# Loading two token rows of a weighted expert sum on 15 DMA engines in place of 16

## The chip, the cores and the metric

The kernel runs on one core of a Trainium2 chip. The metric is the time of the device in microseconds (us), from the start to the end of one execution. The core has five engines with instruction streams of their own: TensorE (PE in the profile), VectorE (DVE), ScalarE (ACT), GpSimd (POOL) and SyncE (SP), which here only issues transfers. Sixteen DMA engines move data between the device's memory (HBM) and the on-chip memory of 128 partitions.

## The reference

Each of 16 x 1024 tokens has eight rows of 512 numbers, one per expert, and eight weights. The output is the weighted sum over the experts.

```python
batch, seq, n_experts, expert_dim = 16, 1024, 8, 512
# expert_outputs: (batch, seq, n_experts, expert_dim), combine_weights: (batch, seq, n_experts)
weights = combine_weights[..., np.newaxis]
return np.sum(expert_outputs * weights, axis=2).astype(np.float32)
```

In float32 the input is 268 MB and the output 34 MB, and each number read is used once.

## The kernel before

The 16384 tokens are laid over the 128 partitions: each partition works on 128 of them, and "token i" below is the i-th of every partition at once, so one token is 128 rows of 16 KB (eight experts of 512 float32). A ring of ten tokens holds the loaded rows. A transfer brings up to four tokens; towards the end they get smaller.

```python
    G = 8
    SLOTS = 10
    PE_TOKENS = 8
    PE_EXPERTS = 3

    x = expert_outputs.rearrange("b s e d -> (b s) e d").rearrange(
        "(n p g) e d -> n p g e d", p=P, g=G
    )
    # ... (weights and output in the same way)
    ring = one.tile([P, SLOTS, E, D], fp32, name="ring")
    acc = one.tile([P, 2 * G, D], fp32, name="acc")
    # ...
    loads = []
    BULK = 112
    t = 0
    while t < BULK:
        m = min(4, SLOTS - t % SLOTS, G - t % G)
        loads += [(t, m, 0, E)]
        t += m
    for t in range(BULK, T_P - 2, 2):
        loads += [(t, 2, 0, E)]
    loads += [(T_P - 2, 1, 0, 4), (T_P - 2, 1, 4, 8)]
    loads += [(T_P - 1, 1, 0, 3), (T_P - 1, 1, 3, 5), (T_P - 1, 1, 5, 7), (T_P - 1, 1, 7, 8)]

    def load_until(t):
        nonlocal loaded
        while loaded < len(loads) and loads[loaded][0] + loads[loaded][1] <= t:
            i, m, e0, e1 = loads[loaded]
            n, g, s = i // G, i % G, i % SLOTS
            if (e0, e1) == (0, E):
                dst, src = ring[:, s : s + m], x[n, :, g : g + m]
            else:
                dst, src = ring[:, s, e0:e1], x[n, :, g, e0:e1]
            pin(nc.sync.dma_start(out=dst, in_=src))
            loaded += 1
```

For all tokens but the last eight, ScalarE makes the first term (row of expert 0 times its weight) and VectorE adds the other seven, one instruction each. For the last eight, TensorE makes the terms of three experts by multiplying with a diagonal matrix of the weights, and VectorE adds five.

```python
    for i in range(0, T_P, 2):
        load_until(i + SLOTS)
        for k in (i + 2, i + 3):
            if k < T_P:
                first(k)              # ScalarE's term, or TensorE's three
        for e in range(E):
            for k in (i, i + 1):
                term(k, e)            # VectorE: acc = ring * weight + acc
        end = i + 2
        if end <= T_P - G and end % G == 0:
            store(end - G, G, nc.scalar)
        # ... (stores of the last eight tokens: 4, 2, 1 and 1)
```

A load waits until the ring's places that it writes have been read by VectorE and ScalarE. Loads go through SyncE's queue, most stores through ScalarE's.

Of the kernel before, what the change touches and what calls it, by code (L numbers as in the profile page):

```python
# [1 line left out]

# [5 lines left out]


@with_exitstack  # L10
def kernel(
    ctx: ExitStack,
    tc: tile.TileContext,
    expert_outputs: bass.AP,
    combine_weights: bass.AP,
    out: bass.AP,
):

    nc = tc.nc
    fp32 = mybir.dt.float32
    mult, add = mybir.AluOpType.mult, mybir.AluOpType.add
    pin = tc.keep_in_program_order

    B, S, E, D = expert_outputs.shape
    T = B * S
    P = 128
    G = 8
    N = T // (P * G)
    T_P = N * G
    SLOTS = 10
    PE_TOKENS = 8
    PE_EXPERTS = 3

    x = expert_outputs.rearrange("b s e d -> (b s) e d").rearrange(
        "(n p g) e d -> n p g e d", p=P, g=G
    )
    w = combine_weights.rearrange("b s e -> (b s) e").rearrange(
        "(n p g) e -> p n (g e)", p=P, g=G
    )
    o = out.rearrange("b s d -> (b s) d").rearrange("(n p g) d -> n p g d", p=P, g=G)

    one = ctx.enter_context(tc.tile_pool(name="one", bufs=1))
    diag_pool = ctx.enter_context(tc.tile_pool(name="diag_pool", bufs=12))  # L50
    ps_pool = ctx.enter_context(
        tc.tile_pool(name="ps_pool", bufs=4, space=bass.MemoryType.PSUM)
    )

    ring = one.tile([P, SLOTS, E, D], fp32, name="ring")
    acc = one.tile([P, 2 * G, D], fp32, name="acc")
    w_t = one.tile([P, T_P, E], fp32, name="w_t")
    ident = one.tile([P, P], fp32, name="ident")


    loads = []
    BULK = 112
    t = 0
    while t < BULK:
        m = min(4, SLOTS - t % SLOTS, G - t % G)
        loads += [(t, m, 0, E)]
        t += m
    for t in range(BULK, T_P - 2, 2):
# [3 lines that stand above are left out]
    loaded = 0  # L72
# [7 lines that stand above are left out]
                dst, src = ring[:, s : s + m], x[n, :, g : g + m]  # L80
            else:
                dst, src = ring[:, s, e0:e1], x[n, :, g, e0:e1]
            pin(nc.sync.dma_start(out=dst, in_=src))  # L83
            loaded += 1

    sums = {}

    def first(i):

        s, a = i % SLOTS, i % (2 * G)  # L90
        if i < T_P - PE_TOKENS:
            pin(nc.scalar.mul(out=acc[:, a], in_=ring[:, s, 0], mul=w_t[:, i, 0:1]))  # L92
            return
        ps = ps_pool.tile([P, D], fp32, name="ps")
        for e in range(PE_EXPERTS):
            diag = diag_pool.tile([P, P], fp32, name="diag")
            pin(nc.scalar.mul(out=diag, in_=ident, mul=w_t[:, i, e : e + 1]))  # L97
            nc.tensor.matmul(  # L98
                ps, lhsT=diag, rhs=ring[:, s, e], start=e == 0, stop=e == PE_EXPERTS - 1
            )  # L100
        sums[i] = ps

    def term(i, e):
        s, a = i % SLOTS, i % (2 * G)
        if i < T_P - PE_TOKENS:
            before, e0 = acc[:, a], 1
        else:
            before, e0 = (sums[i] if e == PE_EXPERTS else acc[:, a]), PE_EXPERTS
        if e >= e0:
            pin(  # L110
                nc.vector.scalar_tensor_tensor(  # L111
                    out=acc[:, a],
                    in0=ring[:, s, e],
                    scalar=w_t[:, i, e : e + 1],
                    in1=before,
                    op0=mult,
                    op1=add,
                )
            )

    def store(i, m, queue):
        n, g, a = i // G, i % G, i % (2 * G)
        pin(queue.dma_start(out=o[n, :, g : g + m], in_=acc[:, a : a + m]))

    pin(nc.sync.dma_start(out=w_t.rearrange("p (n g) e -> p n (g e)", g=G), in_=w))  # L125
    make_identity(nc, ident)
    load_until(SLOTS - 2)
    for i in (0, 1):
        first(i)
# [4 lines that stand above are left out]
                first(k)  # L134
        for e in range(E):
            for k in (i, i + 1):
                term(k, e)
# [3 lines that stand above are left out]
        elif end == T_P - 4:  # L141
            store(end - 4, 4, nc.scalar)
        elif end == T_P - 2:
            store(end - 2, 2, nc.sync)
        elif end == T_P:
            store(end - 2, 1, nc.sync)
            store(end - 1, 1, nc.sync)


# [1 line left out]
_INS = ['expert_outputs', 'combine_weights']  # L151
_OUTS = [((16, 1024, 512), 'float32')]


# [23 lines left out]
```

## Time and profile before

| | |
|---|---|
| time, median of 3 (lowest, highest) | 719.63 us (719.17, 720.88) |
| span of the profiled execution | 718.5 us |
| VectorE busy | 585.6 us (81%), 880 instructions |
| ScalarE busy | 86.7 us (12%) |
| TensorE busy | 28.0 us (4%), in the last 50 us |
| moved by DMA | 302.59 MB, 421 GB/s over the span |
| a load of four tokens, from issue to landing | 35.6 us, median of 19 |
| one VectorE term | 746 ns, 128x512 |

The busy share of an engine says how much of the span it worked, not whether it was waited for. The profile's table of stages gives busy time per engine in a stretch of the span and, in its last two columns, the share of the 16 DMA engines that were busy and the rate. The chain of waits follows the work that ended last back to what released it, step by step. Each DMA queue has a row with its packets, its megabytes and the share of the sixteen engines' span that its packets took. Queue 1 is SyncE's and queue 10 ScalarE's; queue 14 brings instructions. The trace also records when each of the sixteen shares of a transfer had landed.

### The profile page before, as it was taken

How to read it: one execution, taken by the hardware profiler on the slowest of the kernel's cores; microseconds unless marked ns; L12 is line 12 of the kernel's file. 1: busy time of each engine (PE TensorE's matmuls, PEld its weight loads, DVE VectorE, ACT ScalarE, POOL GpSimd, SP SyncE). 2: the span in 40 equal slices, each digit the busy share in tenths (PEclk: the TensorE clock that was granted, in tenths of full speed). 3: DMA queues.
4: the chain of work that ended last, by engine and by line, in shares of the span. 5: the costliest groups of instructions: out<-in, count | busy, mean ns of one | idle time of the engine just before them, and what ended most of it. 6: DMA issues, size and time to landing. Idle time of an engine off the chain costs nothing.

```text
span 718.5 us, 1363 instructions
## 1 busy us (share of the span) xinstructions
PE 28.0 (4%) x48; PEld 11.4 (2%) x48; DVE 585.6 (81%) x880; ACT 86.7 (12%) x145; POOL 0.7 (0%) x6
## 2 busy tenths in 40 slices
PE   0000000000000000000000000000000000000374
PEld 0000000000000000000000000000000000000131
DVE  0499888799697979897789787879897799997647
ACT  0210101111001110101110011111101101102210
POOL 0000000000000000000000000000000000000000
PEclk9999999999999999999999999999999999999967
DMA  9999999999999999999999999999999999999991
GB/s 372 441 427 420 423 438 420 455 406 462 423 425 440 449 405 436 447 431 440 429 415 453 431 425 440 422 430 447 424 441 435 434 416 436 436 431 434 427 405 73
DMA packets 11577, 302.59 MB, mean 421 GB/s; under 512 B 3120, under 2 KB 3120, under 8 KB 4016
## 3 DMA queue, kind: packets, MB, share of 16 engines
q1 hardware_dynamic: 9264, 270.01, 87.3%
q10 hardware_dynamic: 2304, 32.51, 10.6%
q14 instruction: 9, 0.07, 0.0%
HBM read 268.96 MB, written 33.55 MB: 421 GB/s over the span
## 4 chain that ended last, share of the span: by engine, by line
DMA 58%; DVE 36%; PE 2%; ACT 1%; issue 1%; DVEq 0%; SPq 0%; ACTq 0%
DMA ring<-in_expert_outputs_dram 58%; DVE acc L111 36%; PE ps L98 2%; ACT acc L92 1%; ACT L92 0%; DVEq L173 0%; SPq L125 0%; SPq L83 0%; ACTq L92 0%; DVEq L111 0%
## 5 line engine op out<-in xcount | busy, mean ns | idle before, releaser
L111 DVE SCALAR_TENSOR_TENSOR acc<-ring,w_t,acc 128x512 f32<-128x512 f32 x872 | 580.1, 746 | 111.6 <-ACT acc L92 111.6
L92 ACT ACTIVATE acc<-ring,w_t 128x512 f32<-128x512 f32 x120 | 77.6, 711 | 556.6 <-DMA ring<-in_expert_outputs_dram 556.5
L98 PE MATMUL ps<-ring,diag 128*128 128x512 f32 x48 | 28.0, 748 | 679.9 <-DMA ring<-in_expert_outputs_dram 675.7
L98 PEld LDWEIGHTS ps<-ring,diag 128*128 128x128 f32 x48 | 11.4, 245 | 695.6 <-issue 694.1
L111 DVE SCALAR_TENSOR_TENSOR acc<-ring,w_t,ps 128x512 f32<-128x512 f32 x8 | 5.9, 745 | 18.2 <-PE ps L98 18.2
L97 ACT ACTIVATE diag<-ident,w_t 128x128 f32<-128x128 f32 x24 | 7.9, 390 | 29.3 <-PE ps L98 21.8
L92 ACT ACT_TABLE_LOAD x1 | 1.3, 1283 | 25.9 <-DMA ring<-in_expert_outputs_dram 25.9
masks.py:199 POOL TENSOR_SCALAR_AFFINE_SELECT ident<-ident 128x128 f32<-128x128 f32 x1 | 0.3, 292 | 0.1
masks.py:197 POOL MEMSET ident<- 128x128 f32 x1 | 0.2, 205 | 0.3 <-POOLq L162 0.3
L162 POOL MEMSET const-bfloat16-1.0<- 128x1 bf16 x1 | 0.1, 102 | 0.0
L162 POOL MEMSET const-uint8-127<- 128x1 uint8 x1 | 0.1, 102 | 0.0
L162 POOL MEMSET const-float32-0.0<- 128x1 f32 x1 | 0.1, 98 | 0.2 <-issue 0.2
L162 POOL MEMSET const-float32-1.0<- 128x1 f32 x1 | 0.1, 98 | 0.0
## 6 DMA issues: line engine op xcount, KB each, us to landing
ring<-in_expert_outputs_dram SPq DMA_DIRECT2D x19, 4096.0 KB, 35.6
out_dram<-acc ACTq DMA_DIRECT2D x15, 2048.0 KB, 21.9
ring<-in_expert_outputs_dram SPq DMA_DIRECT2D x2, 1024.0 KB, 40.6
ring<-in_expert_outputs_dram SPq DMA_DIRECT2D x2, 512.0 KB, 25.9
out_dram<-acc ACTq DMA_DIRECT2D x1, 1024.0 KB, 7.7
ring<-in_expert_outputs_dram SPq DMA_DIRECT2D x1, 768.0 KB, 41.8
w_t<-in_combine_weights_dram SPq DMA_DIRECT2D x1, 512.0 KB, 4.1
out_dram<-acc SPq DMA_DIRECT2D x1, 512.0 KB, 2.7
```

Source lines behind the costliest of these rows:

```text
L92: pin(nc.scalar.mul(out=acc[:, a], in_=ring[:, s, 0], mul=w_t[:, i, 0:1]))
L97: pin(nc.scalar.mul(out=diag, in_=ident, mul=w_t[:, i, e : e + 1]))
L98: nc.tensor.matmul(ps, lhsT=diag, rhs=ring[:, s, e], start=e == 0, stop=e == PE_EXPERTS - 1)
L111: nc.vector.scalar_tensor_tensor(out=acc[:, a], in0=ring[:, s, e], scalar=w_t[:, i, e : e + 1], in1=before, op0=mult, op1=add,)
L162: nc = _bacc.Bacc("TRN2", target_bir_lowering=False, num_devices=1)
```

## The change

Tokens 48 and 72 are loaded alone, and each in four pieces: partitions 0 to 119, then 120, then 121 and 122, then 123 to 127. A transfer of 120 partitions is meant to run on 15 DMA engines with eight partitions each, so that the sixteenth has nothing to do for it[...]. The neighbours of these tokens in the order of loading are cut differently for it: tokens 48 and 49 were one load and are now two (the first in four pieces), and 72-75 and 76-79 become 72, 73, 74-77 and 78-79. The computation and the stores are the same.

```diff
@@ -36,6 +36,7 @@
     SLOTS = 10
     PE_TOKENS = 8
+    SHORT = (48, 72)
     PE_EXPERTS = 3
@@ -63,6 +64,8 @@
         m = min(4, SLOTS - t % SLOTS, G - t % G)
+        if t in SHORT or t - 1 in SHORT:
+            m = 1
         loads += [(t, m, 0, E)]
         t += m
@@ -80,7 +83,10 @@
-            pin(nc.sync.dma_start(out=dst, in_=src))
+
+            parts = (0, 120, 121, 123, P) if i in SHORT else (0, P)
+            for p0, p1 in zip(parts, parts[1:]):
+                pin(nc.sync.dma_start(out=dst[p0:p1], in_=src[p0:p1]))
             loaded += 1
```

## The prediction

> **What bounds the kernel now.** I read the stages first (busy time of each engine per stretch, granted clock, share of the 16 DMA engines that is busy, and what they moved), then the DMA queues on the page.
>
> ```profile
> core 0: us, PE busy (x) PEld busy (x) DVE busy (x) ACT busy (x) POOL busy (x), PEclk, DMA share, GB/s
> 100.00:300.00 200.00, 0.00 (x0) 0.00 (x0) 168.00 (x254) 24.47 (x38) 0.00 (x0) 1.00 1.00 432
> 300.00:500.00 200.00, 0.00 (x0) 0.00 (x0) 170.17 (x257) 23.25 (x36) 0.00 (x0) 1.00 1.00 434
> 500.00:690.00 190.00, 14.35 (x24) 5.83 (x24) 159.00 (x239) 25.48 (x48) 0.00 (x0) 0.98 1.00 431
> 690.00:700.00 10.00, 5.79 (x8) 2.53 (x8) 6.28 (x10) 1.86 (x6) 0.00 (x0) 0.68 1.00 410
> 700.00:707.00 7.00, 7.00 (x17) 3.04 (x16) 4.78 (x8) 0.00 (x0) 0.00 (x0) 0.97 0.13 53
> 707.00:718.50 11.50, 0.85 (x2) 0.02 (x1) 8.40 (x13) 0.00 (x0) 0.00 (x0) 0.66 0.24 91
> ...
> q1 hardware_dynamic: 9264, 270.01, 87.3%
> q10 hardware_dynamic: 2304, 32.51, 10.6%
> q14 instruction: 9, 0.07, 0.0%
> ```
>
> Until 700 us the DMA engines are busy the whole time (share 1.00); VectorE, the busiest compute engine, has 168 us of work in 200. So the transfers set the pace. A 64 KB load packet takes 2.418 us in the packet records, 27.1 GB/s for one engine, and 16 of these are 434 GB/s: the rate in the table. But from 700 to 707 us the share is 0.13, two engines' worth in the mean. Something is still moving when nearly all have finished.
>
> What that is, the completion marks tell: each transfer leaves sixteen in the trace, one per share. I list them for some loads (tokens, and when the 1st, 8th, 15th and 16th share landed, us):
>
> ```
> tokens   8- 9    52.85   53.26   54.67   54.90
> tokens  48-49   271.26  271.65  273.35  273.80
> tokens  72-75   411.58  412.01  413.67  415.06
> tokens  96-99   542.20  542.62  544.26  547.64
> tokens 124-125  687.55  688.02  689.81  694.02
> token  127 end  697.61  698.03  699.82  706.39
> ```
>
> Fifteen shares land within 1.8 to 2.3 us of each other all the way; some nine come early, the rest up to 2 us later. The sixteenth falls behind, from 0.2 us after the fifteenth to 4.2 at tokens 124-125 and 6.6 at the end. The marks have no engine number, but it is one engine, for its lag grows in equal steps. The packets of the queue of kind "instruction" (8 KB each) start at 70.3, 157.1, 250.0, 278.1, 355.6, 443.6, 538.9, 586.6 and 631.9 us. After those at 157, 250, 356, 444, 539 and 632 one load packet is about 0.65 us longer, and with the fetch's own 0.31 one share is later by 0.96 to 0.98. They come some 95 us apart, which is 128 VectorE instructions of 0.746 us: VectorE's instruction stream, fetched through one DMA engine. Six steps of 0.97 are 5.8; with its place at the start (0.5 after the first) 6.4, and 694.02 - 687.55 is 6.47.
>
> Last, the end of the chain of waits (start, length, what):
>
> ```profile
> 682.63 7.44 PE ps L98 x12
> 690.07 0.02 issue
> 690.09 4.07 DVE acc L111 x6
> 694.16 0.10 issue
> 694.27 8.44 PE ps L98 x12
> 702.71 0.03 issue
> 702.74 4.79 DVE acc L111 x8
> ```
>
> TensorE starts tokens 124-127 at 694.27. The chain names VectorE, but the matmul waits for several semaphores: the PSUM buffer it needs from VectorE was read at 674.3 (token 120), and the load of tokens 124-125 landed at 694.02. So the late engine's share releases it. From there to the end all is compute: 718.5 - 694.0 = 24.5 us (24 matmul passes in 13.6 us, the rest of VectorE's terms, a store). The last pieces of token 127, landed at 706.39, are needed only after 710 and bind nothing. What counts is when tokens 124-125 are complete.
>
> [...]
>
> **The change part by part.** Bytes, VectorE, ScalarE and TensorE instructions stay as they are.
>
> *Issue.* Tokens 48-49 become 5 loads in place of 1, tokens 72-79 seven in place of 2: 9 more issues of 0.33 us on SP, 3 us on an idle sequencer. Loads wait about 35 us from issue to landing, so the queue has some 30 us of work at any time, and this is hidden. The eight completion counters rotate faster; I followed who reuses which. The closest is token 73's load, whose counter belonged to tokens 64-67, landed by 371.5 us; its buffer comes free at about 370. A us or two, hidden too.
>
> *Taken from engine 15.* Eight rows of 16 KB per token. A 16 KB packet of the stores takes 0.611 us, so 8 x 0.611 = 4.9 us per token, 9.8 us for both. If the late engine is 15, it goes from 6.47 us behind the first to 3.3 ahead of it.
>
> *Given to others.* [...] Engine 0: 2 x 3 x 0.611 = 3.7 us; engine 1: 2.4; the others 1.2.
>
> *Sum.* The load of tokens 124-125 is complete when its last engine is. If engine 0 is among the early ones, that is 687.55 + 3.7 + 0.2 = 691.4, beside 689.8 for the late fifteen: 694.0 - 691.4 = 2.6 us gained, and as only compute follows, the end moves as much: 717.0. If the single row is spread over 16, engine 0 gets 2.06 rows per token, 2.5 us, and the landing is 690.1: 3.9 gained, 715.7.
>
> **Rivals.** *Engine 0 is one of the later group:* 687.55 + 2.3 + 3.7 = 693.5, only 0.5 gained, 719.1. The uneven split 1, 2, 5 [...] suggests that it was fitted to engines with slack; this speaks against.
>
> *The late engine is not 15:* if it is one that gets nothing, 719.6; if it is engine 0, 719.6 + 3.7 = 723.3. [...]
>
> [...] Two in step would then need twice the 4.9 us. In the worst case 9.8 us for both tokens on nearly all engines, less about twice their offset (up to 2 us) per token: tokens 124-125 at 698 to 701, a time of 724 to 727. Nothing in the profile before speaks for or against it, as all its transfers have 128 rows. I give it a quarter.
>
> *Already hidden:* if the end hung on VectorE rather than on that landing, nothing would move. VectorE idles 3.63 us before 699.77 and 2.22 before 702.74, both waits on TensorE, so there is no such reserve.
>
> **Range and chances.** About half for 715.5 to 717.5, a quarter for 718.5 to 720.5, a quarter for 721 to 727. I take 717.6, a little above the sum, with 714.9 to 723.5. Two per cent are 14.4 us; nothing here reaches that, save a conflict that disturbs neighbouring loads too.
>
> **What would show it.** Right: the sixteenth mark is no longer apart, the spread at tokens 124-125 under 4 us, their landing near 691, and the low DMA share after 700 gone. The marks of the 120-row loads spread no wider than others. Wrong engine: the lag of 6.5 is still there or has become 10. Conflict: the first fifteen shares land later after tokens 48 and 72, by up to 5 us each, and packets of 16 KB take about 1.2 us where 0.61 was expected.

## The result, and the profile after

The changed kernel is slower: 738.36 us (median of 4 runs, 737.94 to 740.65) beside 720.25 (719.17 to 721.10). The ratio is 1.0259, with a 95% interval of 1.0232 to 1.0286. The prediction of 717.6 us, with 714.9 to 723.5 as its range, does not hold.

The table of stages of the changed kernel, with the columns as before (busy time of each engine, granted clock, share of the 16 DMA engines that is busy, GB/s):

```profile
100.00:300.00 200.00, 0.00 (x0) 0.00 (x0) 163.57 (x246) 22.02 (x34) 0.00 (x0) 1.00 1.00 418
300.00:500.00 200.00, 0.00 (x0) 0.00 (x0) 158.47 (x238) 22.13 (x34) 0.00 (x0) 1.00 1.00 413
500.00:690.00 190.00, 1.72 (x2) 0.84 (x3) 167.57 (x252) 26.22 (x46) 0.00 (x0) 1.00 1.00 433
690.00:700.00 10.00, 6.72 (x11) 2.47 (x9) 3.99 (x6) 3.15 (x9) 0.00 (x0) 1.00 0.99 428
700.00:711.00 11.00, 7.08 (x12) 2.79 (x12) 6.44 (x11) 0.00 (x0) 0.00 (x0) 0.84 0.97 411
711.00:736.70 25.70, 13.34 (x24) 5.56 (x24) 16.57 (x25) 1.86 (x6) 0.00 (x0) 0.71 0.34 135
```

The DMA engines are as busy as before (share 1.00), but between 100 and 500 us they move less: 418 and 413 GB/s, where it was 432 and 434. After 500 us the rate is the old one. So the time goes where tokens 48 and 72 pass, and it goes in transfers that take longer, not in waiting for something to transfer. Five-microsecond windows around token 48 show it; first the kernel before, then the changed one:

```profile
265.00:270.00 5.00, 0.00 (x0) 0.00 (x0) 5.00 (x9) 1.09 (x2) 0.00 (x0) 1.00 1.06 459
270.00:275.00 5.00, 0.00 (x0) 0.00 (x0) 5.00 (x9) 1.12 (x2) 0.00 (x0) 1.00 1.05 452
```

```profile
265.00:270.00 5.00, 0.00 (x0) 0.00 (x0) 3.74 (x6) 2.56 (x4) 0.00 (x0) 1.00 1.00 223
270.00:275.00 5.00, 0.00 (x0) 0.00 (x0) 5.00 (x9) 0.00 (x0) 0.00 (x0) 1.00 0.99 226
```

For ten microseconds the engines are fully busy at half the rate. The packet records agree: the 512 load packets of 16 KB (tokens 48 and 72, and 49 and 73 queued right behind them) last 1.15 us in the median, where 0.61 was expected.

The same loads as in the prediction's list of completion marks (when the 1st, 8th, 15th and 16th share landed, us), as far as both kernels have them:

```
                         1st      8th     15th     16th
tokens  50-53 before  291.85   292.27   294.57   294.96
              after   296.22   300.69   302.55   304.70
tokens  80-83 before  455.09   455.51   457.18   459.54
              after   463.55   472.06   474.79   478.01
tokens 124-125 before 687.55   688.02   689.81   694.02
              after   699.87   703.35   707.26   712.42
```

After token 48 the middle of the engines is 8.4 us late, after token 72 16.5, at the end 15.3. One share is ahead of the next by 3.3 and then 7.1 us. I take it for the engine that the two loads of 120 rows leave out (each left completion marks for fifteen shares, not sixteen), the prediction's engine 15; eight missing rows per token would make at most 4.9 and 9.8 (an estimate, 8 and 16 packets of 0.611 us). No record names an engine, so every engine number here and in the recorded texts is the author's. And the sixteenth share is still apart from the rest: at tokens 124-125 it lands 9.1 us after the eighth, where it was 6.0. The last engine was not relieved.

The end of the chain of waits of the changed kernel hangs on that landing as before:

```profile
666.22 46.20 DMA ring<-in_expert_outputs_dram
712.42 0.24 issue
712.66 8.21 PE ps L104 x12
720.87 0.02 issue
720.89 4.79 DVE acc L117 x8
```

From 712.42 to the end of the span, 736.7, it is 24.3 us (24.5 before). The landing came 18.4 us later and the time is 18.1 us longer. Two questions follow: why all engines lose some 15 us, and why the late one loses another 3.

### The profile page after: what moved, and what is told of

Read it like the earlier page. It is cut to its first block, busy times and chain, and to the rows that moved or that the text cites. A ratio compares the mean times of both kernels' runs of the same rounds, so it can differ in the third digit from the quotient of the medians.

```text
span 736.7 us, 1389 instructions
## 1 busy us (share of the span) xinstructions
PE 28.9 (4%) x48; PEld 11.7 (2%) x48; DVE 585.7 (80%) x880; ACT 87.0 (12%) x145; POOL 0.7 (0%) x6
## 3 DMA queue, kind: packets, MB, share of 16 engines
q10 hardware_dynamic: 2304, 32.51, 10.3%
## 4 chain that ended last, share of the span: by engine, by line
DMA 60%; DVE 36%; ACT 1%; issue 1%; PE 1%; DVEq 0%; SPq 0%; ACTq 0%
DMA ring<-in_expert_outputs_dram 60%; DVE acc L117 36%; PE ps L104 1%; ACT acc L98 1%; ACT L98 0%; DVEq L179 0%; SPq L131 0%; SPq L89 0%; DVEq L117 0%; ACTq L98 0%
```

## The experiments

The prediction's rival of engines that hinder each other when they write at the same moment (two in step, twice the time) fits the halved rate of 223 and 226 GB/s, but so would others: the order of the reads in HBM, an odd number of engines, the small pieces, the finer cut. The first four runs tell them apart; their expectations give first what this conflict would make, then what the others would.

**Loads alone.** Eight one-token loads ahead of the kernel before, each starting when the one before has landed, and five tiny transfers behind the load of tokens 118-119 that count the engines off.

```diff
+    marks = one.tile([16, 5, 128], fp32, name="marks")
 ...
             pin(nc.sync.dma_start(out=dst, in_=src))
             loaded += 1
+            if i == 118:
+                for k in range(1, 6):
+                    pin(nc.sync.dma_start(out=marks[:k, k - 1], in_=x[0, :k, 0, 0, :128]))
 ...
+    row = x[0, :, 0]
+    for dst, src in (
+        (ring[:, 0], row),
+        (ring[0:120, 0], row[0:120]),
+        (ring[0:126, 0], row[0:126]),
+        (ring[0:64, 0], row[0:64]),
+        (ring[0:120, 0], x[0, :15].rearrange("p g e d -> (p g) e d")),
+        (ring[0:127:9, 0], row[0:127:9]),
+        (ring[0:15, 0], row[0:15]),
+        (ring[:, 0], row),
+    ):
+        pin(nc.sync.dma_start(out=dst, in_=src))
     load_until(SLOTS - 2)
```

> The kernel before, with eight loads of one token ahead of its own, each starting when the one before has landed, so that all engines begin together: 128 rows, 120, 126, 64, 120 from HBM rows that lie one after the other, 15 rows nine partitions apart, the first 15 rows, 128 again. Also five tiny transfers of 1, 2, 3, 4 and 5 rows behind the load of tokens 118-119. [...] packets of 16 KB take 0.61 us in the loads of 128, in that of 126 [...] and of 15 spaced rows; 1.2 us in both loads of 120 and in that of 64; the first 15 rows[...], about 2.4 us. So 120 rows take 4.9 us longer than 128, and 64 rows as long as 128. HBM theory (the order of the reads there collides): the load of 120 from consecutive rows is fast again, and 64 and 15 rows are like 128. Odd-count theory (a transfer that isn't 16 shares is slow): 120, 126 and both loads of 15 rows are slow, 64 isn't. The tiny transfers tell the late engine's number: I expect its late mark in those of 4 and 5 rows and not in those of 1 to 2[...].

The time of the whole, 783.26 us in one run, contains the added loads and says nothing. The windows from each load's issue to its last landing (second column, us) do; in order 128 rows (the first of all, beside the load of the weights), 120, 126, 64, 120 from consecutive HBM rows, 15 spaced, the first 15, and 128 again:

```profile
1.24:10.89 9.65, 0.00 (x0) 0.00 (x0) 0.00 (x0) 0.00 (x0) 0.06 (x1) 1.00 0.80 272
10.91:22.55 11.64, 0.00 (x0) 0.00 (x0) 0.00 (x0) 0.00 (x0) 0.00 (x0) 1.00 0.78 169
22.57:30.58 8.01, 0.00 (x0) 0.00 (x0) 0.00 (x0) 0.00 (x0) 0.00 (x0) 1.00 0.67 258
30.59:38.04 7.45, 0.00 (x0) 0.00 (x0) 0.00 (x0) 0.00 (x0) 0.00 (x0) 1.00 0.65 141
38.06:50.13 12.07, 0.00 (x0) 0.00 (x0) 0.00 (x0) 0.00 (x0) 0.00 (x0) 1.00 0.75 163
50.15:53.38 3.23, 0.00 (x0) 0.00 (x0) 0.00 (x0) 0.00 (x0) 0.00 (x0) 1.00 0.26 76
53.39:57.32 3.93, 0.00 (x0) 0.00 (x0) 0.00 (x0) 0.00 (x0) 0.00 (x0) 1.00 0.29 63
57.40:64.60 7.20, 0.00 (x0) 0.00 (x0) 0.00 (x0) 0.00 (x0) 0.00 (x0) 1.00 0.76 291
```

120 rows take 11.64 us, 128 rows 7.20: 4.4 more for less data. 64 rows take 7.45, about as long as 128. With 126 rows it is 8.01, near 7.20 and one more row of 0.61 on each engine, as 14 engines with nine rows would need (an estimate). It fits the packets under 512 B, one per share (16 in the last load of 128 rows, 15 in the first of 120): of the 137 such packets that this run has over the kernel before (3257 and 3120), 60 are left for the four loads of 126, 64, 15 and 15 rows, and 14, 16, 15 and 15 are 60. Consecutive HBM rows change nothing (12.07). The median packet of 16 KB lasts 0.61 us with 128 and 126 rows, 1.26 to 1.28 with 120 and 64. So it isn't the order in HBM, nor, by these counts, leaving engines out; and 15 rows need 1.57 us from first packet to last landing when they are spaced and 2.99 when they are the first 15, so it isn't the odd number either. It is which partitions are written at the same time.

Why some sets of partitions are slow together was not shown: no record says which engine wrote which row, nor how the 128 rows of a load are divided.

Two readings show that engines slowing each other in pairs are not the whole of it. Fifteen can't all be paired, yet all fifteen shares of the 120 rows landed between 22.27 and 22.55 us, and no packet took less than 0.90 us or more than 1.29. It looks as if an engine without a partner is slowed as well; how stays open. And the packets of the first 15 rows were expected to take 2.4 us and show 1.25 in the median. Those rows need 1.4 us more than the spaced ones, somewhat less than the 1.8 that three more packets of 0.611 would make.

The marks of the tiny transfers tell which engine is late. Each leaves one mark just after issue and then one per share; the last landed at 716.08 us (1 row), 716.73 (2), 716.91 (3), 723.46 (4) and 723.64 (5). The jump of 6.55 us comes with the fourth row: a transfer of four rows has a share on the late engine, and one of three has none. Counted from 0 in this order, it is **engine 3**; that is a name for what the marks show. The mark of five rows was as late, so I take it that in the changed kernel the piece of five rows gives this engine one row more for each of the two tokens. That the 120 rows take none from it fits the sixteenth share, 9.1 us behind the eighth, where it was 6.0.

**The cut alone.**

```diff
-            parts = (0, 120, 121, 123, P) if i in SHORT else (0, P)
+            parts = (0, P)
```

> The changed kernel, with its finer cut of the loads (48, 49, 72, 73 alone, 74-77, 78-79), but tokens 48 and 72 as single transfers of 128 rows. [...] the cut itself costs nothing, 719 to 721 us. If the small packets of 16 KB, or the issue of more loads, are the cost, it stays near 738.

720.16 us (12 runs), ratio to the kernel before 1.0001 [0.9990, 1.0012]. Three of the nine additional loads are in this run, and they cost nothing that can be measured, nor does the rotation of the completion counters that comes with them.

**The eight rows in one transfer.**

```diff
-            parts = (0, 120, 121, 123, P) if i in SHORT else (0, P)
+            parts = (0, 120, P) if i in SHORT else (0, P)
```

> The changed kernel, with the eight rows left over in one transfer [...] in place of three of 1, 2 and 5. [...] nearly all of the loss stays, 733 to 738 us; it drops by up to 2 us [...]. If the three small pieces and their queueing are the cost: 719 to 723.

739.75 us (736.72 to 744.45, 4 runs), ratio 1.0258 [1.0234, 1.0282]: as slow as with three pieces, and above the 733 to 738 expected. The uneven split is not the cause.

**Two halves.**

```diff
-            parts = (0, 120, 121, 123, P) if i in SHORT else (0, P)
+            parts = (0, 64, P) if i in SHORT else (0, P)
```

> The changed kernel, with tokens 48 and 72 loaded as two transfers of 64 rows each[...]. [...] about 4.9 us are lost per token on every engine, 728 to 732 us, with the late engine's lag as before the change. If 15 in place of 16 engines, or the small pieces, are the cost: 719 to 721.

738.06 us (733.10 to 745.19, 4 runs), ratio 1.0226 [1.0170, 1.0282]. No load of 120 rows is in it and no piece of a few rows, and the loss is the same. (A load of 64 rows has sixteen shares, if the packets of the loads alone are divided as above.) So writing half of the partitions at a time makes such a loss by itself; but it is about 9 us per token where 4.9 were worked out, with a wide spread.

**In the stream.** Why is it more than the 4.4 us of a load alone? Six sequences of four queued one-token loads, all engines starting together, with only the second load different. The first times expected are for a loss that carries over into the loads behind, the others for one that stays inside the token.

```diff
+    whole, last = (0, P), 0
+    for second in ((0, P), (0, 120), (0, 64, P), (0, 120, P), (0, 126, P), (0, P)):
+        for j, parts in enumerate((whole, second, whole, whole)):
+            s = (last + j) % 4
+            for p0, p1 in zip(parts, parts[1:]):
+                pin(nc.sync.dma_start(out=ring[p0:p1, s], in_=x[0, p0:p1, j]))
+        last = (last + 3) % 4
     load_until(SLOTS - 2)
```

> The kernel before, with six sequences of four one-token loads ahead of its own, each sequence starting when the one before has landed, the loads within it queued without a wait. Only the second load differs: 128 rows; 120; 64 and 64; 120 and 8; 126 and 2; 128 again. Alone, 120 rows cost 4.4 us more than 128, but in the changed kernel each such token costs 7 to 9 us. [...] the sequences with 120 and with 64 and 64 are 6 to 8 us longer than those of 128 from first issue to last landing; the one of 126 and 2 is only 0.5 to 2 longer. If only the collisions inside the token count, it is 4 to 5 for 120 and for 64 and 64, and the rest of the loss in the kernel comes from elsewhere: stores beside it, or engines already out of step when it starts.

The whole took 877.38 us in one run, with the sequences in it. The windows of the sequences (128; 120; 64 and 64; 120 and 8; 126 and 2; 128), and last a stretch inside the fourth, where the eight rows left over pass:

```profile
1.24:25.19 23.95, 0.00 (x0) 0.00 (x0) 0.00 (x0) 0.00 (x0) 0.06 (x1) 1.00 0.93 372
25.21:52.32 27.11, 0.00 (x0) 0.00 (x0) 0.00 (x0) 0.00 (x0) 0.00 (x0) 1.00 0.92 305
52.34:79.21 26.87, 0.00 (x0) 0.00 (x0) 0.00 (x0) 0.00 (x0) 0.00 (x0) 1.00 0.94 312
79.23:108.77 29.54, 0.00 (x0) 0.00 (x0) 0.00 (x0) 0.00 (x0) 0.00 (x0) 1.00 0.93 284
108.79:136.95 28.16, 0.00 (x0) 0.00 (x0) 0.00 (x0) 0.00 (x0) 0.00 (x0) 1.00 0.90 298
136.97:159.04 22.07, 0.00 (x0) 0.00 (x0) 0.00 (x0) 0.00 (x0) 0.00 (x0) 1.00 0.92 380
...
94.50:97.50 3.00, 0.00 (x0) 0.00 (x0) 0.00 (x0) 0.00 (x0) 0.00 (x0) 1.00 1.16 153
```

Against the last sequence (22.07): 120 rows cost 5.0 us, 64 and 64 cost 4.8, and 120 with the eight rows 7.5. Two of the last kind are 14.9, near the 15.3 by which the middle of the engines is late in the changed kernel. So the 120 rows are about two thirds (5.0 of 7.5), and the eight rows add 2.4 us, as long as four packets of 0.611 us one after the other; why they take so long was not shown. While they pass, the rate falls to 153 GB/s, and the sixteen packets that start between 95.3 and 97.0 us last 1.95 to 2.60 us. At most eight of these packets are of the eight rows, so the others are held up too. Why was not settled. And 126 with 2 rows, fast alone (8.01 us for the 126), costs 6.1 in the stream (28.16 in place of 22.07); why was not shown.

**One token.**

```diff
-    SHORT = (48, 72)
+    SHORT = (48,)
```

> The changed kernel with token 48 alone in four pieces; token 72 and its neighbours as before. If each such token pays its own price in the stream: half of the loss, 728 to 730 us. If the first throws the engines out of step for good and the second adds little: 734 to 738.

727.77 us (4 runs), ratio 1.0111 [1.0094, 1.0127]: 7.8 us for the first token, which leaves 10.3 of the 18.1 for the second. Each pays in the stream, the second somewhat more.

**The eight rows in four pairs.** A transfer of two rows had no late mark in the run of loads alone (716.73 us, where four rows had 723.46), so these should give engine 3 no row more.

```diff
-            parts = (0, 120, 121, 123, P) if i in SHORT else (0, P)
+            parts = (0, 120, 122, 124, 126, P) if i in SHORT else (0, P)
```

> The changed kernel with the eight rows left over as four transfers of two rows[...], so that engine 3, found to be the late one, gets none of them. [...] Engine 3's lag behind the middle of the others at tokens 124-125 was 6.0 us before and about 9 after the change; it should be 6 to 8 here, and the time 735 to 738 us. If it was only the extra rows on engines 0 to 4 that made the kernel slower, the time is about 725.

740.55 us (4 runs), ratio 1.0289 [1.0273, 1.0304]: slower still, and the expectation of a gain fails. At tokens 124-125 two shares are apart now, 7.4 and 8.3 us after the eighth, and the eighth itself is 19.0 us later than before the change. Which of the two is engine 3 can't be told. With the eight rows in pairs all the others came later, too: 3.7 us at the eighth share, beside the changed kernel.

**A store issued later.** A test of what sets the end, on the kernel before.

```diff
-        if end <= T_P - G and end % G == 0:
+        if end < T_P - G and end % G == 0:
             store(end - G, G, nc.scalar)
         elif end == T_P - 4:
+            store(T_P - 2 * G, G, nc.scalar)
             store(end - 4, 4, nc.scalar)
```

> The kernel before, with all its loads in 128 rows; only the store of tokens 112-119 is issued later, together with that of 120-123. What binds the end is the landing of tokens 124-125 on engine 3; this store puts 8 rows of 16 KB, 4.9 us, on every engine ahead of that landing. Theory that this landing sets the end: it comes up to 4.9 us earlier, 715 to 717 us. If the end hangs on the last bytes moved by any engine, or on VectorE: 719 to 721.

719.37 us (12 runs), ratio 0.9995 [0.9987, 1.0004]: nothing gained. The marks say why. The store went out at 679.44 us, and at tokens 124-125 the eighth share came 3.7 us earlier than before (684.29 beside 688.02), but the sixteenth at 694.16 (694.02). The late engine still had its share of these tokens to move and took the store in between. The end follows the last engine and not the others.

**Fewer instruction fetches.** On the kernel before; the output lacks the terms of experts 5, 6 and 7 for the first 120 tokens.

```diff
-        if e >= e0:
+        if e >= e0 and (i >= T_P - PE_TOKENS or e < 5):
```

> The kernel before, but VectorE leaves out the terms of experts 5, 6 and 7 for the first 120 tokens: 360 of its 880 instructions are not there, all transfers are the same, and the output lacks these terms. VectorE is not what the kernel waits for, so this only takes away instruction fetches: 520 instructions need three fewer of 128. If these fetches make engine 3 late and its lag sets the end: the lag at tokens 124-125 goes from 6.5 us to about 3.6 and the time to 716.5 to 717.5. If the lag comes from something else: 719 to 721.

716.88 us (5 runs), ratio 0.9943 [0.9925, 0.9961]. From the page of this run, VectorE's busy time and the queue that brings instructions:

```profile
PE 27.8 (4%) x48; PEld 11.2 (2%) x48; DVE 348.1 (49%) x520; ACT 86.8 (12%) x145; POOL 0.7 (0%) x6
...
q14 instruction: 6, 0.05, 0.0%
```

Six packets in place of nine, and a time as expected, although VectorE never set the pace. But in the trace the sixteenth share of tokens 124-125 landed at 693.04 us, 5.3 after the first (6.5 before), not 3.6. The marks say why. The late engine's share is 1.2 us behind the first before the packet at 95.7 us, and 2.1, 3.2, 4.2 and 5.2 behind it after the packets at 95.7, 244.7, 419.9 and 575.1 us; between these it grows only for a while, where a store runs beside the loads. That is again a step of about 1.0 after each fetch of VectorE's instructions, but four of them, where six made the engine later in the kernel before: two fewer, not three, and from a start 0.7 us later (1.2 in place of 0.5). So the fetches account for the growth of the lag. The time is less clear: of the 2.3 us by which this span is shorter than the one before, 1.0 is the earlier landing, and 1.3 the first twelve matmuls behind it, which took 7.10 us in place of 8.44 for a reason that isn't shown:

```profile
693.29 7.10 PE ps L98 x12
```

Loads were also issued earlier (43.3 us from issue to landing, where it was 35.6). The forecast of the time came true partly by luck.

**The store behind the late share.**

```diff
-        if end <= T_P - G and end % G == 0:
+        if end < T_P - G and end % G == 0:
             store(end - G, G, nc.scalar)
         elif end == T_P - 4:
             store(end - 4, 4, nc.scalar)
+            store(T_P - 2 * G, G, nc.scalar)
```

> The kernel before, with the store of tokens 112-119 issued right after the one of 120-123. When it was issued just ahead of it (at 679 us), engine 3 still moved it ahead of its late share of tokens 124-125, which landed at 694.16, as before (694.02). Issued after about 691 us, it lies behind that share on engine 3 too. If that landing sets the end: it lands 4 to 5 us earlier and the time is 714.5 to 717. If engine 3 then gets the last pieces of token 127 too late, the gain is smaller, 717 to 719.

714.74 us (714.20 to 715.89, 4 runs), ratio 0.9925 [0.9907, 0.9943]. This is 5.2 us faster than the kernel before, with the whole computation in it and every load in 128 rows. Tokens 124-125 are complete at 690.06, 4.0 us earlier. The end of its chain of waits:

```profile
670.60 0.02 issue
670.62 32.95 DMA ring<-in_expert_outputs_dram
703.57 0.03 issue
703.60 0.02 DVEq L111
703.62 0.01 issue
703.63 0.09 DVE acc L111
```

Now a piece of token 127, whose last share (the late engine's, as I take it) landed at 703.57, is what VectorE waits for: the next bound, which was hidden before.

**Without the eight rows.** Rows 120-127 of tokens 48 and 72 are not loaded and keep what lay there.

```diff
-            parts = (0, 120, 121, 123, P) if i in SHORT else (0, P)
+            parts = (0, 120) if i in SHORT else (0, P)
```

> The changed kernel without the loads of rows 120-127 of tokens 48 and 72 (256 KB are not moved, and these rows keep what lay there, so the output is off in them). In the sequences, 120 rows cost 5.0 us more than 128 and the eight left over[...], 2.4 more. If the kernel adds up the same way: the middle of the engines comes 10 us later at tokens 124-125 than before the change, engine 3's lag behind it stays about 6, and the time is 729 to 732 us. If the eight rows are only a small part of the loss: 735 to 738.

734.08 us (731.94 to 739.67, 4 runs), ratio 1.0203 [1.0157, 1.0249]. The eight rows would be about 4 of the 18 us, in line with 2 x 2.4, but the intervals of the two kernels overlap; the 120 rows alone cost 14, or 7 per token, not 5, and the time is above the 729 to 732 expected. In the profiled run, the longest of the four, the last share, engine 3's as I take it, was 13.5 us behind the eighth, though this kernel gives it no extra row. It was 13.4 in the run with one piece of eight rows and 13.7 in that of two halves. So the late engine can lose more than the others without an extra row, and why it loses 3 us more in the changed kernel stays open; its two additional rows are 1.2 of them.

**Later tokens.** Does a token cost more when the late engine is further behind?

```diff
-    SHORT = (48, 72)
+    SHORT = (80, 104)
```

> The changed kernel with tokens 80 and 104 in place of 48 and 72, the rest of its rule the same. When 48 and 72 pass, engine 3 is 0.4 and 1.4 us behind the other fifteen in the kernel before; when 80 and 104 pass, it is about 2.4 and 3.3 behind. If an engine that runs behind collides with more of the loads queued after the token[...]: engine 3 ends later than the 12.4 us of the changed kernel behind the first mark's engine at the end or about 9 behind the middle, and the time is 741 to 747 us. If the price of such a token doesn't depend on that: 737 to 740.

736.61 us (735.37 to 742.00, 4 runs), ratio 1.0248 [1.0202, 1.0294]. The idea falls: in the kernel before, the late engine is further behind where these tokens pass (2.4 and 3.3 us in place of 0.4 and 1.4), and they cost no more.

## Why the prediction was wrong

**What bounds the kernel.** Right. The landing of tokens 124-125 on one late engine sets the end: in the changed kernel that landing moved by 18.4 us and the time by 18.1, and the two late stores show it from both sides.

**The fetches.** Right: with four fetches in place of six the late share again steps back by about 1.0 us after each, and at no other place for good.

**"If the late engine is 15".** This step failed. The late engine is the one that a fourth row brings in (716.91 us with three rows, 723.46 with four), named engine 3 here. That it was the one left out was the author's estimate from the shape of the change, and no measurement of this kernel. The engine left out became the first, by 3.3 and 7.1 us, and engine 3 got a row more per token (inferred from the mark of five rows). The prediction's rivals had no engine that is late and gets one row; by its own sum that makes 719.6 + 1.2 = 720.8 us (an estimate), so this step alone takes away the gain but doesn't make the kernel slower by 18 us.

**The number of engines.** Right as to their number: in the trace of the changed kernel the four pieces of each token left completion marks for 15, 1, 2 and 5 shares, those of token 48 between 270.79 and 277.11 us. The single row left one and was not spread. (For a spread row the prediction's sum gives 690.2, not 690.1, which changes nothing.) Which engines these are no record tells; that one engine has a row of each of the three small pieces, 3.7 us for both tokens, was the author's estimate.

**The sum.** This step failed too, and it was the larger error: it took each moved row at 0.611 us and the 120 rows at their old speed. Their packets take 1.26 us alone, twice that, and the two halves, with no load of 120 rows, lose as much as the changed kernel (738.06 us). The rival of two engines in step, given a quarter, had the right size of packet (about 1.2 us, where the changed kernel's median is 1.15); its worst case was 9.8 us for both tokens "less about twice their offset". Measured, a token in this shape costs 7.5 us in a queue of loads and 7.8 to 10.3 in the kernel. What was left out: the eight remaining rows cost 2.4 us per token in the queue, and packets beside theirs are held up as well (sixteen of 1.95 to 2.60 us); and offsets between engines did not lessen the loss. The rest, some 1.6 us per token between the queue of loads and the kernel, stays open. Engine 3's lag at the moment when the token passes was tested as its cause and made no difference; a store running at the same time, or the engines' offsets of up to 2 us when the token starts, were not tested.

**Already hidden, and issue.** Right as far as it was tested: the finer cut of the loads, with three of the nine more issues and its order of counters, costs nothing (ratio 1.0001). The issues of the pieces were not tested apart.

## What to carry to other kernels

A transfer on 15 engines is not a transfer with one engine spared: what counted here is which partitions are written at the same moment, and of the shapes tried only the load of 128 rows was fast both alone (7.20 us) and in a queue of loads (22.07 us for four). When one DMA engine ends late, find out which it is before relieving it, with tiny transfers of 1, 2, 3... rows behind a large one, and look for the count at which the last mark jumps (here four rows, by 6.55 us). And when the last landing sets the end, look at what else is queued ahead of it on that engine: a store that could wait until after it gained 5.2 us, and moving rows lost 18.

## What was not expected of the hardware

- While the eight rows left over passed, the sixteen packets of 16 KB that started between 95.3 and 97.0 us lasted 1.95 to 2.60 us and the rate was 153 GB/s, less than beside the 120 rows (223 to 226 in the kernel).
- In the load of 120 rows all fifteen shares were slow alike (0.28 us between the first and the last landing), although fifteen can't all be in pairs. The shortest packet took 0.90 us, where the median of the 128 rows is 0.61.
- 126 rows took 8.01 us alone, near the 7.20 of 128 rows, but cost 6.1 us more in a queue of loads.
- VectorE's instruction stream has a price in a kernel that waits for transfers: 0.96 to 0.98 us of one DMA engine each time, some 95 us apart in the kernel before, about every 128 instructions of 0.746 us (an estimate).
